# A hybrid attention, mLSTM and PEER layer on one core: 32 first products ahead in place of 28, four of them at the hand-over, and 18 lower parts on GpSimd

## The chip, the core and the metric

The kernel runs on one core of a Trainium2 chip. The metric is the device time of one execution in microseconds. Three timed executions of the kernel before gave a median of 1732.3 us (1725.78 to 1736.87). TensorE is called PE below, VectorE DVE, ScalarE ACT, GpSimd POOL, and SyncE, which issues most DMAs, SP.

## The reference, cut to what matters

The layer has an attention part and an mLSTM part, which come first and which the change doesn't touch. What follows them is PEER: for each token and each of 8 heads, two lists of 16 best sub-keys are ranked, their 256 sums are ranked again, and the 16 best pairs name 16 of 16384 experts.

```
def peer(h, w_pq, sub_keys, expert_u, expert_v):
    ...
        q = (xb @ w_pq).reshape(PEER_BLOCK, PEER_HEADS, 2, PEER_DKH)
        s = jnp.einsum('thpd,hpkd->thpk', q, sub_keys).astype(jnp.float32)
        sv, si = lax.top_k(s, PEER_TOPK)
        cand = (sv[:, :, 0, :, None] + sv[:, :, 1, None, :]).reshape(PEER_BLOCK, PEER_HEADS, -1)
        ...
        best, pos = lax.top_k(cand, PEER_TOPK)
        eidx = jnp.take_along_axis(cidx, pos, axis=-1)
        g = jax.nn.softmax(best, axis=-1)
        act = jax.nn.gelu(jnp.einsum('thkd,td->thk', expert_u[eidx], xb).astype(jnp.float32), approximate=False)
        return jnp.einsum('thk,thkd->td', (g * act).astype(xb.dtype), expert_v[eidx])
```

There are 512 tokens, 1024 channels, 8 heads, 128 keys to a list and 16384 experts.

## The kernel before

Of the four tiles of 128 tokens, tiles 1 to 3 (384 tokens) take PEER densely. The 16384 experts are 128 chunks of 128. For chunk c the **first product** multiplies the chunk of `expert_u` by the 384 tokens (`dense_u`, 24 matmuls of 384 columns, into the one PSUM buffer `u`); Gelu follows on ACT; `weigh` multiplies by the gates of the chunk (DVE, L1271); the **second product** multiplies by the chunk of `expert_v` and adds into six PSUM banks `o` (`dense_v`, 18 matmuls of 512 columns, L1283). Every operand is a pair of a rounded upper part (a copy on ACT, L218) and a lower part (the difference, L219), and `mm3` issues three matmuls for a pair of operands (upper by upper, L255; upper by lower, L256; lower by upper, L257). `split` makes both parts; its last argument is the engine of the difference, DVE if it isn't given. Tile 0 takes PEER sparsely: its lists are ranked by DVE (`tile0`, the generator `late`), and then 256 rows of `expert_u` and `expert_v` are gathered and used one after the other (`gathered`, the generator `gath`).

In time the program has these stages after attention:

- The query products of tiles 1 to 3 (to about 483 us), in which DVE begins to rank (`best16`: MAX8, FIND_INDEX8, MATCH_REPLACE8, MAX8, FIND_INDEX8).
- **Routing** (to about 743 us). Two calls of `weave` mix three strands each, in the given proportions: the ranking on DVE (`first`, `second`), the work of tile 0 on PE, and the first products ahead (`pre`). `second` also makes the gates: one-hot tables on DVE (L1181 to L1186), products on PE (`g`, L1196), evictions on ACT (L1198) into one of two buffers `sg`, and stores to `gd` in HBM in four quarters (L1203, issued by ACT). CFG `f` holds the weights of the strands and how many first products go with each; CFG `pre` is how many are done ahead in all. Outside of `manual_schedule` a scheduler orders each engine's instructions; inside it they stand as they are written.
- **The hand-over.** The gates of the first four chunks come back from `gd` (`load_g`, L1249), the first chunks of `expert_v` are loaded (`load_v`, L1254) into a ring of two buffers `vt`, chunk 0 is weighed and split, and the second products begin. The first buffer of `vt` lies on the last quarter of the buffer `sg` that the last gates are stored from.
- **Second products alone**: while c is below PRE - 1, the chunk's first product is already done. `turn` issues the 47 steps of `late` here, evenly spaced from L0 to G0 (CFG `l`).
- **Pairs**: one first product and one second product for each chunk, with the gathers of tile 0 spread between them.

SP issues its DMAs in order and waits, in order, for what each of them needs. A step of `late` fetches the next list (64 KB from `sc0d`, L1293) into a ring of two buffers and ranks the one before.

Of the kernel before, what the change touches and what calls it, by code (L numbers as in the profile page):

```python
# [49 lines left out]
ENDED = object()  # L50
CFG = dict(nv=2, r=8, l=(0, 34, 124), pre=28, f=(17, 7, 7, 27, 2, 4), oa=2, og=2, gt=2, a=(0, 2), ps=(('g', 2), ('j', 1), ('b', 2), ('s', 1)), w=(22, 22, 22), ko=(4, 5, 6, 7, 0, 1, 2, 3), m=(5, 7, 4, 7, 4, 4, 1), ne=lambda v, g: g, sc=lambda k, n: n == 256 or k % 2, wq=lambda nc: nc.sync, we=lambda i, v, g: g)


class Arena:
# [71 lines left out]
def body(ctx, tc, nc, x_t, ctx_t, cc, w_ada_t, w_ada_n, w_in, w_uq, w_ukv, w_out, w_pq, keys_t,  # L126
# [90 lines left out]
    def split(hi, lo, src, eng=V):  # L217
        A.activation(hi, src, AF.Copy)  # L218
        eng.tensor_tensor(lo, src, f32(hi), op=OP.subtract)  # L219
# [820 lines left out]
    PRE = CFG["pre"]  # L1040
    utr, uhr, ulr = ar.ring("ut", 2, [KD, P]), ar.ring("uh", 3, [4, P], F32R), ar.ring("ul", 3, [4, P], F32R)
    gep = []
# [7 lines left out]
    def split_u(c_, half):  # L1050
        if c_ < P and (c_, half) not in us:
            us[c_, half] = uhr.next(), ulr.next()
            split(*us[c_, half], uts[c_][:, 4 * half:4 * half + 4])

    def dense_u(c_, half):
        if c_ < P and (c_, half) not in fired:
# [163 lines left out]

    def tail0():
        yield from tile0_q()
        yield from pre

    weave((first(), 52), (tile0_x(), CFG["f"][0]), (islice(pre, CFG["f"][1]), CFG["f"][2]))
    obr, ogr = ar.ring("ob", 1, [8, P, 2], BF), ar.ring("og", CFG["og"], [2, 8, P, 2], F16)
    sgr = ar.ring("sg", 2, [P, 32])
    weave((second(), 170), (tail0(), CFG["f"][3]), (islice(pre, CFG["f"][4]), CFG["f"][5]))
    assert len(gep) == PRE
    front.close()  # L1230
    pso = pool(ctx, "pso", 1, **PS)
    ob = [pso.tile([P, 512], F32, name="o%d" % i) for i in range(6)]
# [140 lines left out]

    with tc.manual_schedule():
        NV = len(vtr.v)
        load_g(0)
        for c_ in range(NV):
            load_v(c_)
        load_g(4)
        weigh(0)  # L1380
        weigh_lo(0)
        split_v(0, 0)
        split_v(0, 1)
        for c_ in range(P):
            if c_ == PRE:
                ar.give(*["gp%d" % i for i in range(PRE)])
                tl.update(rows=ar.ring("rows", CFG["r"], [D]), act=ar.take("act", [P]), acc=ar.take("acc", [D]),
                          h2t=ar.take("h2t", [D]))
                nc.scalar.dma_start(tl["h2t"], h0d)
            dense_u(c_ + 1, 0)  # L1390
            split_u(c_ + 2, 0)
            dense_u(c_ + 1, 1)
            split_u(c_ + 2, 1)
            load_u(c_ + 3)
            turn(c_, 1)
            weigh(c_ + 1)
            if c_ < P - 1:
                dense_v(c_, 0)
            turn(c_, 2)
            split_v(c_ + 1, 0)  # L1400
            if c_ < P - 1:
                dense_v(c_, 1)
            else:
                for g in range(3):
                    for half in range(2):
                        dense_v(c_, half, (g,))
            split_v(c_ + 1, 1)
            weigh_lo(c_ + 1)
            load_v(c_ + NV)
            if c_ % 4 == 3:  # L1410
                load_g(c_ + 5)
            turn(c_, 3)
        for _ in late:
            pass
        for _ in gath:
            pass
# [93 lines left out]
```

## Time and profile before

| | |
|---|---|
| median of three executions | 1732.3 us |
| the profiled execution, its own time | 1736.11 us |
| its span | 1734.3 us |
| PE busy | 1629.1 us (94%) |
| DVE busy | 1332.7 us (77%) |
| ACT busy | 735.3 us (42%) |
| POOL busy | 443.6 us (26%) |
| share of the chain that ended last | PE 72%, DVE 17%, ACT 4%, DMA 4% |

Busy shares are means over stages that have different limits, so the stages have to be read one by one. The profiled execution is 3.8 us above the median, and 1.8 us of its time lie outside of its span.

### The profile page before, as it was taken

To read this page: it belongs to the slowest core of one execution; us is meant where nothing else is said; L and a number is where in the kernel's file an instruction comes from. 1 tells how busy PE (TensorE), PEld (TensorE's weight loads), DVE (VectorE), ACT (ScalarE), POOL (GpSimd) and SP (SyncE) were. 2 spreads that over 40 slices of the span, in tenths; PEclk is the share of its full clock that TensorE was granted. 3 is DMA by queue.
4 is the path that set the end of the run, shared out by engine and by line. 5 is a ranking of instruction groups with operands and counts; after the bars stand their busy time and mean duration, and the time that the engine had idled before them with its cause. 6 is when DMAs were issued, how large, how long until landed. Compare 5 with 4: busy or idle time off the path is not lost.

```text
span 1734.3 us, 25190 instructions
## 1 busy us (share of the span) xinstructions
PE 1629.1 (94%) x9119; PEld 1412.4 (81%) x9119; DVE 1332.7 (77%) x2857; ACT 735.3 (42%) x1404; POOL 443.6 (26%) x339
## 2 busy tenths in 40 slices
PE   6889999998988999969899999999999999999988
PEld 4669854588968989857689999999999999999977
DVE  6896165556899997958876887888888888888874
ACT  4563544434345545534353433333333333334322
POOL 6621400033400000000101333333333434444311
PEclk8999988999999999989999999999999999999989
DMA  8456301133314757565777999999999999999962
GB/s 340 145 184 218 104 25 37 31 110 122 119 50 170 267 214 256 204 202 162 260 237 214 341 321 335 336 328 322 325 339 322 318 343 331 323 335 334 314 226 82
DMA packets 155244, 400.92 MB, mean 231 GB/s; under 512 B 13424, under 2 KB 70192, under 8 KB 150000
## 3 DMA queue, kind: packets, MB, share of 16 engines
q1 hardware_dynamic: 108320, 232.05, 39.0%
q0 software_dynamic: 36864, 134.23, 22.5%
q10 hardware_dynamic: 9936, 33.03, 4.9%
q8 instruction: 71, 1.16, 0.3%
q14 instruction: 53, 0.43, 0.1%
HBM read 367.28 MB, written 31.99 MB: 230 GB/s over the span
## 4 chain that ended last, share of the span: by engine, by line
PE 72%; DVE 17%; ACT 4%; DMA 4%; issue 2%; POOL 0%; ACTq 0%; SPq 0%; DVEq 0%
PE o L1283 27%; PE u L255 9%; PE u L257 9%; PE u L256 9%; PE j L255 2%; PE j L256 2%; PE j L257 2%; DVE sp L219 2%; PE s L846 1%; DVE sp L1186 1%; PE s L847 1%; PE g L1196 1%; ACT sp L218 1%; DMA sp<-in_exp_ut 1%; DMA sp<-in_w_ada_t 1%
## 5 line engine op out<-in xcount | busy, mean ns | idle before, releaser
L218 ACT ACTIVATE sp<-sp 128x512 fp32r<-128x512 f32 (+2 forms) x674 | 406.4, 637 | 465.5 <-PE u L256 257.5
L1283 PE MATMUL o<-sp 128*128 128x512 f32 x2304 | 550.1, 393 | 21.1 <-ACT sp L218 14.9
L219 DVE TENSOR_TENSOR sp<-sp,sp 128x512 fp32r<-128x512 f32 (+1 forms) x650 | 407.6, 658 | 158.7 <-ACT sp L218 158.6
L1283 PEld LDWEIGHTS o<-sp 128*128 128x128 f32 x2304 | 432.1, 189 | 113.4 <-ACT sp L218 15.8
L255 PE MATMUL u<-sp,sp 128*128 128x384 f32 x1024 | 349.2, 341 | 14.1 <-ACT sp L1269 7.8
L257 PE MATMUL u<-sp,sp 128*128 128x384 f32 x1024 | 347.8, 340 | 6.7 <-DVE sp L219 6.7
L256 PE MATMUL u<-sp,sp 128*128 128x384 f32 x1024 | 346.1, 338 | 0.0
L1347 POOL DMA_INDIRECT sp<-in_exp_u,sp x128 | 137.2, 1072 | 679.2 <-PE o L1283 360.0
L255 PEld LDWEIGHTS u<-sp,sp 128*128 128x128 f32 x1024 | 194.0, 189 | 20.9 <-ACT sp L1074 8.4
L1347 POOL DMA_INDIRECT sp<-in_exp_v,sp x128 | 151.9, 1187 | 222.3 <-DVE sp L1323 204.9
L257 PEld LDWEIGHTS u<-sp,sp 128*128 128x128 f32 x1024 | 193.7, 189 | 9.0 <-DVE sp L219 7.9
L256 PEld LDWEIGHTS u<-sp,sp 128*128 128x128 f32 x1024 | 193.8, 189 | 3.9
L219 POOL TENSOR_TENSOR sp<-sp,sp 128x2048 fp32r<-128x2048 f32 (+1 forms) x24 | 96.5, 4024 | 264.6 <-ACT sp L218 264.6
L1323 DVE SCALAR_TENSOR_TENSOR sp<-sp 128x1024 f32<-128x1024 f32 x127 | 162.5, 1279 | 0.2
L1311 DVE CUSTOM_DVE_ANT_0 sp<-sp 128x1024 f32<-128x1024 f32 x128 | 155.6, 1215 | 0.0
L257 PE MATMUL j<-sp,sp 128*128 128x256 f32 (+2 forms) x448 | 140.7, 314 | 5.0 <-DVE sp L398 5.0
L255 PE MATMUL j<-sp,sp 128*128 128x256 f32 (+2 forms) x448 | 143.0, 321 | 1.7 <-ACT sp L218 0.9
L256 PE MATMUL j<-sp,sp 128*128 128x256 f32 (+2 forms) x448 | 141.0, 315 | 0.0
L1269 ACT ACTIVATE sp<-u 128x384 f32<-128x384 f32 x100 | 49.2, 492 | 173.4 <-PE u L257 160.5
L1271 DVE TENSOR_TENSOR sp<-sp,sp 128x384 f32<-128x384 f32 x107 | 61.2, 572 | 63.2 <-ACT sp L1269 46.3
L257 PEld LDWEIGHTS j<-sp,sp 128*128 128x128 f32 x448 | 84.6, 189 | 7.5 <-DVE sp L398 5.7
L255 PEld LDWEIGHTS j<-sp,sp 128*128 128x128 f32 x448 | 84.8, 190 | 6.0 <-issue 1.7
(343 smaller groups left out, 1804.3 us busy)
## 6 DMA issues: line engine op xcount, KB each, us to landing
sp<-in_exp_ut SPq DMA_DIRECT2D x128, 512.0 KB, 5.4
sp<-in_exp_v SPq DMA_DIRECT2D x128, 512.0 KB, 6.3
gd<-sp ACTq DMA_DIRECT2D x48, 512.0 KB, 4.5
sp<-gd SPq DMA_DIRECT2D x32, 768.0 KB, 9.7
sp<-in_w_ada_t SPq DMA_DIRECT2D x38, 512.0 KB, 4.4
sp<-in_w_pq SPq DMA_DIRECT2D x16, 1024.0 KB, 5.1
sp<-in_w_in SPq DMA_DIRECT2D x8, 1024.0 KB, 5.2
sp<-in_w_out SPq DMA_DIRECT2D x8, 1024.0 KB, 4.8
```

Source lines behind the costliest of these rows:

```text
L218: A.activation(hi, src, AF.Copy)
L219: eng.tensor_tensor(lo, src, f32(hi), op=OP.subtract)
L255: T.matmul(ps, lh, rh, start=(first and i == 0), stop=False)
L256: T.matmul(ps, lh, rl, start=False, stop=False)
L257: T.matmul(ps, ll, rh, start=False, stop=(last and i == n - 1))
L846: T.matmul(p_[:, c0:c1], qn[:, h, o], knT[:, h, c0:c1], start=True, stop=False)
L1269: A.activation(ge, pu.pop(c_), AF.Gelu)
L1271: V.tensor_tensor(blk(w), blk(ge), gts[c_ // 4][:, :, c_ % 4], op=OP.mult)
L1283: T.matmul(ob[2 * g + half], l_[:, g * P:g * P + P], fl(r_), start=(c_ == 0 and i == 0), stop=(c_ == P - 1 and i == 2))
L1311: V.tensor_tensor_reduce(out=u, in0=u, in1=h2t, scale=1.0, scalar=0.0, op0=OP.mult, op1=OP.add, accum_out=act[:, j:j + 1])
L1323: V.scalar_tensor_tensor(acc, v, act[:, j:j + 1], acc, op0=OP.mult, op1=OP.add)
L1347: G.indirect_dma_start(out=r_, out_offset=None, in_=table, in_offset=bass.IndirectOffsetOnAxis(ap=col, axis=0))
```

## The change

PRE becomes 32 and `hold` is 4: 28 first products still lie in the two calls of `weave` (now 9, 17 and 2 in its strands, before 7, 19 and 2), and four more are written into the hand-over, each followed by two steps of `late`. The loads of the first two chunks of `expert_v` are written ahead of these four, the first two loads of gates behind them. For the first nine chunks `split_u` takes the difference on POOL. In CFG `l` the second number goes from 34 to 36. The table PLACE, which says where each buffer lies in SBUF, changes for buffers of this stage; the buffers `vt`, `sg` and `gt` lie where they lay.

```
-CFG = dict(nv=2, r=8, l=(0, 34, 124), pre=28, f=(17, 7, 7, 27, 2, 4), ...
+CFG = dict(nv=2, r=8, l=(0, 36, 124), pre=32, hold=4, f=(17, 9, 9, 25, 2, 4), ...
...
     def split_u(c_, half):
         if c_ < P and (c_, half) not in us:
             us[c_, half] = uhr.next(), ulr.next()
-            split(*us[c_, half], uts[c_][:, 4 * half:4 * half + 4])
+            split(*us[c_, half], uts[c_][:, 4 * half:4 * half + 4], G if c_ < CFG["f"][1] else V)
...
     def tail0():
         yield from tile0_q()
-        yield from pre
+        yield from islice(pre, PRE - CFG["hold"] - CFG["f"][1] - CFG["f"][4])
...
-    assert len(gep) == PRE
+    assert len(gep) == PRE - CFG["hold"]
...
     with tc.manual_schedule():
         NV = len(vtr.v)
-        load_g(0)
+
         for c_ in range(NV):
             load_v(c_)
+        for _ in pre:
+            for _ in range(2):
+                done[1] += 1
+                next(late)
+        split_v(0, 0)
+        split_v(0, 1)
+        load_g(0)
         load_g(4)
         weigh(0)
         weigh_lo(0)
-        split_v(0, 0)
-        split_v(0, 1)
```

The lines of the changed kernel are one higher than before from PLACE on. On SP, from the last loads of `expert_ut` on, the kernel before has this order at the hand-over (`gd` are gates, `sc0d` lists of tile 0):

```order
L1048 DMA sp_1707<-in_exp_ut 128x1024 x15
L1249 DMA sp_58<-gd 128x12x128
L1254 DMA sp_58<-in_exp_v 128x1024 x2
L1249 DMA sp_58<-gd 128x12x128
L1293 DMA sp_3680<-sc0d 128x128
```

The changed kernel has this one there, behind the same 15 loads of `expert_ut`:

```order
L1255 DMA sp_58<-in_exp_v 128x1024 x2
L1049 DMA sp_1707<-in_exp_ut 128x1024
L1294 DMA sp_3680<-sc0d 128x128
L1294 DMA sp_58<-sc0d 128x128
L1049 DMA sp_1707<-in_exp_ut 128x1024
L1294 DMA sp_3680<-sc0d 128x128
L1294 DMA sp_58<-sc0d 128x128
L1294 DMA sp_3680<-sc0d 128x128
L1294 DMA sp_58<-sc0d 128x128
L1294 DMA sp_3680<-sc0d 128x128
L1294 DMA sp_58<-sc0d 128x128
L1250 DMA sp_58<-gd 128x12x128 x2
```

The load of the first gates has moved from the front of this row to its end, behind two loads of `expert_ut` and eight fetches of lists.

On DVE the kernel before has this order at the hand-over (128x2048 are one-hot tables, 128x384 the weighed chunk, 128x512 lower parts of `expert_u` and then of `expert_v`):

```order
L1186 TENSOR_TENSOR sp_58<-sp_58 128x2048 x2
L219 TENSOR_TENSOR sp_3676<-sp_1707,sp_3676 128x512
L1271 TENSOR_TENSOR sp_58<-sp_1707,sp_58 128x384
L219 TENSOR_TENSOR sp_3676<-sp_58,sp_3676 128x384
L219 TENSOR_TENSOR sp_3676<-sp_58,sp_3676 128x512 x2
```

The changed kernel has this one after its last one-hot table; the row goes on in the same way, with two rankings between the lower parts of one held product and those of the next, up to seven rankings:

```order
L1187 TENSOR_TENSOR sp_58<-sp_58 128x2048 x2
L220 TENSOR_TENSOR sp_3676<-sp_1707,sp_3676 128x512 x2
L988 MAX sp_58<-sp_3680 128x8
L989 MAX_INDEX sp_1707<-sp_58,sp_3680 128x8
L990 MATCH_REPLACE sp_58<-sp_58,sp_3680 128x128
L991 MAX sp_58<-sp_58 128x8
L992 MAX_INDEX sp_1707<-sp_58 128x8
L220 TENSOR_TENSOR sp_3676<-sp_1707,sp_3676 128x512 x2
```

Rankings of tile 0 now stand between the lower parts of held products, the first of them ahead of the second product's lower parts.

## Rows read from the trace of the kernel before

**Rows 1.** Windows by stage: span, then busy us per engine, granted clock, DMA share, GB/s.
```profile
480.00:640.00 160.00, 142.08 (x1093) 129.58 (x1092) 157.25 (x595) 81.04 (x169) 0.00 (x0) 0.98 0.51 179
640.00:743.00 103.00, 99.75 (x874) 92.27 (x871) 84.47 (x89) 56.22 (x110) 0.00 (x0) 1.00 0.59 212
743.00:757.00 14.00, 0.27 (x1) 0.27 (x1) 1.40 (x3) 1.90 (x4) 0.00 (x0) 0.60 0.92 303
757.00:881.00 124.00, 116.83 (x485) 91.93 (x486) 106.40 (x362) 48.82 (x93) 7.71 (x8) 0.98 0.68 213
881.00:1660.00 779.00, 779.00 (x3942) 709.43 (x3941) 631.61 (x967) 304.97 (x568) 281.10 (x248) 1.00 0.92 319
```
**Rows 2.** Chain of work that ended last, at the hand-over: start, us, what.
```profile
742.35 1.09 ACT sp L1198 x2
...
745.84 5.58 DMA gd<-sp
...
751.49 4.54 DMA sp<-in_exp_v
...
756.73 4.52 PE o L1283 x9
```
**Rows 3.** Timeline of SP's queue at the hand-over.
```profile
747.15 0.38 SPq L1249 DMA_DIRECT2D sp<-gd  x1
751.49 0.81 SPq L1254 DMA_DIRECT2D sp<-in_exp_v  x2
```
**Rows 4.** Waits of SP's queue from 735 to 790: us in total, times, longest.
```profile
SPq L1254 <- DMA gd<-sp: 3.9, 1, 3.9
```
**Rows 5.** Timeline of DVE behind the hand-over, in brackets the idle time before.
```profile
754.76 0.56 DVE L1271 TENSOR_TENSOR sp<-sp,sp 128x384 f32<-128x384 f32 x1 [16.91 <-DMA sp<-gd]
...
763.02 0.29 DVE L987 MAX8 sp<-sp 128x8 f32<-128x128 f32 x1
...
764.60 0.54 DVE L1271 TENSOR_TENSOR sp<-sp 128x384 f32<-128x384 f32 x1
```
**Rows 6.** Timeline of PE at the first pair.
```profile
881.41 0.33 PE L255 MATMUL u<-sp,sp 128*128 128x384 f32 x1
...
885.60 4.28 PE L1283 MATMUL o<-sp 128*128 128x512 f32 x18
889.72 0.33 PE L255 MATMUL u<-sp,sp 128*128 128x384 f32 x1
```
**Rows 7.** Timeline of PE at the first product ahead.
```profile
490.02 0.69 PE L257 MATMUL u<-sp,sp 128*128 128x384 f32 x1 [4.77 <-DVE sp L219]
```
**Rows 8.** Groups by line: POOL's lower parts of 128x512, busy us, mean ns, idle before.
```profile
L219 POOL TENSOR_TENSOR sp<-sp,sp 128x512 fp32r<-128x512 f32 x6 | 10.5, 1760 | 3.8 <-ACT sp L218 3.8
```
**Rows 9.** The line L219 on POOL: min/median/max ns, first and last start.
```profile
L219 POOL TENSOR_TENSOR sp<-sp,sp x24: 1295/4584/7429, 24.7 to 465.1; 128x2048 fp32r<-128x2048 f32 x18, 128x512 fp32r<-128x512 f32 x6
```
**Rows 10.** Timeline of POOL, its last lower part.
```profile
465.06 4.58 POOL L219 TENSOR_TENSOR sp<-sp,sp 128x2048 fp32r<-128x2048 f32 x1 [5.29 <-ACT sp L218]
```
**Rows 11.** Timeline of DVE from 450 to 482.
```profile
454.63 0.46 DVE L938 TENSOR_TENSOR sp<-sp 128x48 f32<-128x48 f32 x4
465.34 4.87 DVE L938 TENSOR_TENSOR sp<-sp 128x8 f32<-128x8 f32 x7
```
**Rows 12.** Groups by line, of DVE and of ACT: busy us, mean ns, idle before.
```profile
L219 DVE TENSOR_TENSOR sp<-sp,sp 128x512 fp32r<-128x512 f32 x514 | 344.4, 687 | 153.9 <-ACT sp L218 153.8
L218 ACT ACTIVATE sp<-sp 128x512 fp32r<-128x512 f32 x520 | 324.3, 627 | 433.0 <-PE u L256 257.5 <-PE o L1283 153.3 <-DMA sp<-in_exp_v 10.4
L1074 ACT ACTIVATE sp<-u 128x384 f32<-128x384 f32 x28 | 13.7, 488 | 35.7 <-PE u L257 32.5 <-PE j L1135 3.1
```
**Rows 13.** The fetches of lists, L1293: issue to landing, whole run.
```profile
DMA to landing us min/median/max: 1.9/3.9/7.7
```
**Rows 14.** The loads of gates, L1249: issue to landing, whole run.
```profile
DMA to landing us min/median/max: 5.9/9.7/13.3
```
**Rows 15.** Waits of PE from 756 to 890: us in total, times, longest.
```profile
PE o L1283 <- DVE sp L219: 5.9, 8, 1.4
```

More of the change, by code (lines that the diff above doesn't have):

```diff
@@ L44 @@
     24640, 24608, 1405, 16476, 912, 1278, 1549, 16468, 1166, 1421, 1318, 1956, 16688, 1006, 1830,
[2 rows of a table removed]
[2 rows of a table added]
     856, 16497, 1599, 880, 28672, 1038, 576, 704, 24736, 24800, 24968, 25000, 24768, 24888, 16560,
[2 rows of a table removed]
[3 rows of a table added]
 ENDED = object()
-CFG = dict(nv=2, r=8, l=(0, 34, 124), pre=28, f=(17, 7, 7, 27, 2, 4), oa=2, og=2, gt=2, a=(0, 2), ps=(('g', 2), ('j', 1), ('b', 2), ('s', 1)), w=(22, 22, 22), ko=(4, 5, 6, 7, 0, 1, 2, 3), m=(5, 7, 4, 7, 4, 4, 1), ne=lambda v, g: g, sc=lambda k, n: n == 256 or k % 2, wq=lambda nc: nc.sync, we=lambda i, v, g: g)
+CFG = dict(nv=2, r=8, l=(0, 36, 124), pre=32, hold=4, f=(17, 9, 9, 25, 2, 4), oa=2, og=2, gt=2, a=(0, 2), ps=(('g', 2), ('j', 1), ('b', 2), ('s', 1)), w=(22, 22, 22), ko=(4, 5, 6, 7, 0, 1, 2, 3), m=(5, 7, 4, 7, 4, 4, 1), ne=lambda v, g: g, sc=lambda k, n: n == 256 or k % 2, wq=lambda nc: nc.sync, we=lambda i, v, g: g)
 class Arena:
```

9 rows, old and new, of the table PLACE are left out of this document.

## The prediction

> **What bounds the kernel now.** I read the windows by stage first. In the pairs PE is busy for all of the 779 us at full clock, and DVE for 631.6 of them [rows 1], so PE bounds that stage and what leaves PE there leaves the time. A first product takes 4.19 us of it (881.41 to 885.60) and a second product 4.12 us (885.60 to 889.72) [rows 6]. In routing both are near their limit: up to 640 us DVE is busy for 157.3 of 160 us and PE for 142.1; after that PE for 99.8 of 103 us and DVE for 84.5 [rows 1]. The one wide hole of PE is the hand-over, 14 us with 0.27 us of work at a mean granted clock of 0.60 [rows 1]. The chain there runs from the last evictions of gates (end 743.44) over the stores by ACT, the last of which lands at 751.42, to the load of `expert_v`, and PE starts at 756.73 [rows 2]. The first gates were requested at 747.15, before the last store had landed, and used at 754.76 [rows 3, 5]; the request for `expert_v` stood 3.9 us waiting for that last store [rows 4], since its buffer lies on what is stored. So the reader is to see that SP's queue is open until 751.42 only for what doesn't need that buffer.
>
> **Part 1: four first products fewer in the pairs.** 100 pairs become 96, and four second products stand alone in their place: 4 x 4.19 = -16.8 us [rows 6]. The gathers of tile 0 now lie on 90 chunks instead of 93. DVE's 631.6 of 779 us become some 3% denser in them, and PE's 779 of 779 still cover that; without that cover each chunk would run at DVE's pace, which is under 8.31 us by these rows. Counted at nothing.
>
> **Part 2: the hand-over, and what SP and DVE have queued there.** The load of `expert_v` now stands at the head of SP's queue, so all behind it waits until the last store has landed: two loads of `expert_ut`, eight fetches of lists, and then only the gates. I count from 743.44. The store lands at +8.0 [rows 2]. Two issues of `expert_v` take 0.81 us, and the issues behind them about 0.38 us each [rows 3], so the first list is asked for at about +9.6. It lands 1.9 to 7.7 us later [rows 13]; three loads of half a megabyte stand ahead of it, so I take the median of the run, 3.9: +13.5. DVE ranks it before it makes the lower parts of the second held product. One ranking is 1.6 us (763.02 to 764.60) [rows 5], one lower part 0.69 us [rows 12], so PE, which has had the first held product and two matmuls of the second for a cover, goes on at +15.8. It has then stood for about ten microseconds. After the hole before, the first nine matmuls of 512 columns took 4.52 us [rows 2], and nine of eighteen at full clock are 2.06 [rows 6]; I add these 2.5 us. The 22 matmuls left are 22/24 of 4.19, 3.84 us: +22.1.
>
> The third and fourth held products each wait for Gelu of the one before, since the copies of the next upper parts stand behind it on ACT: 0.49 + 0.63 + 0.69 = 1.8 us [rows 12], and then 3.84 us of PE. The rankings between them (two of 1.6 us) fit into that. So the third ends at +27.7, and the fourth has its first lower part at +29.5 and its second at +30.2. The fifth ranking after it (1.6 us) frees the buffer for the eighth fetch, and only behind that fetch are the gates asked for: about +32.2. They landed 7.6 us after their request before (747.15 to 754.76) [rows 3, 5]; that gives +39.8. The product by the gates (0.56 us) [rows 5] and the copy (about 0.5 us, nearest row Gelu of the same width [rows 12]) bring the second products to +40.9. Before it was +13.3 (756.73 less 743.44) [rows 2], so the stage costs **+27.6 us**. Its ends: with the fastest fetch (-2.0), the fastest load of gates, 5.9 us (-1.7) [rows 14] and no slow clock (-2.5), +21.4; with the slowest fetch (+3.8) and the median load of gates, 9.7 us (+2.1), +33.5. I take the middle sum, since every duration in it but the fetch is the nearest one in place. PE does its four products, but stands for about as long as before again, ahead of the second products. The slow clock at their start is in both kernels.
>
> **Part 3: second products alone.** Seven rankings, 7 x 1.6 = 11.2 us of DVE, have left a stage in which DVE is busy for 106.4 of 124 us [rows 1] and PE waits for it 8 times, 5.9 us in all [rows 15]. The other 39 steps keep nearly their old spacing, with the same tables and the same first gathers, and four chunks more have their waits. I take a quarter of the 5.9 us: **-1.5 us**; at most -5.9, and +0.9 (four chunks more at 5.9 us in 27) if nothing is saved.
>
> **Part 4: routing, and the lower parts on POOL.** The first product ahead stood 4.77 us at its first lower part, which was queued on DVE behind rankings. POOL's queue holds nothing ahead of it by then: -4.8 us [rows 7]. DVE gives up 18 x 0.69 = 12.4 us [rows 12]. Against that stands what POOL's instructions do to DVE. Seven additions on DVE that should take about 0.8 us (four larger ones took 0.46 [rows 11]) took 4.87 us when POOL had begun a lower part of 4.58 us 0.3 us before [rows 10, 11]. So an operation of DVE with two operands in SBUF stands until POOL's is over. A lower part of 128x512 takes POOL 1.30 us at least and 1.76 in the mean [rows 8, 9]. The hold for one is therefore between 0 (DVE is at a reduction or a MAX8, which read one operand) and 1.76 us; I take 0.8, a little under the middle, since such operations are mixed among the additions. 18 x 0.8 = 14.4 us eat the 12.4 us; the 2.0 us that remain pass to the end of routing by about half, as PE is the fuller engine after 640 us [rows 1]. Together -4.8 + 1.0, about **-4 us**, with ends at -11 (no hold, and half of the 12.4 us counts) and +14.5 (each is held for 1.76 us, and all of it counts: 31.7 - 12.4 - 4.8).
>
> By the Trainium skill, SBUF — State Buffer, section "Who interferes with whom", a DVE instruction with two inputs in SBUF contends with a GpSimd instruction that reads SBUF, and whichever starts first keeps the shared ports for the whole instruction. The row of 4.87 us beside 4.58 us agrees. Applied to every one of the 18, it would make part 4 the +14.5 us of the upper end, and it speaks against this half of the change; that result is the second rival below.
>
> **Sum.** -16.8 + 27.6 - 1.5 - 4 = +5.3 us. On the profiled execution's 1736.1 us that is 1741.4; that execution is 3.8 us above the median, so the forecast is 1732.3 + 5.3 = 1737.6, about **1738 us**: no change that a measurement can tell (under 1% for this kernel).
>
> **Rival 1: the held products fill the hole.** If SP's queue isn't closed by the last store, because `expert_v` can be loaded before it, lists come at once. The first held product, of which some 18 matmuls stand behind the last gate products, ends at about +2.5, when ACT has issued its last store (745.84 [rows 2]); with 1.8 us of Gelu, copy and lower part and 3.84 us of PE each, the second ends at +8.1 and the third at +13.8, the fourth has its lower parts at +16.3, and behind a ranking, the request, the gates' 7.6 us and 1.1 us more the second products start at about +27, +13.7 on before. With -11 in routing the sum is -16.8 + 13.7 - 1.5 - 11 = -15.6: 1717 us. The place of the buffer speaks against it [rows 4]; 12%, of which some more than half ends beyond 1% faster if the waits of part 3 go too.
>
> **Rival 2: POOL holds DVE up.** Each of the 18 lower parts holds a two-operand operation of DVE for the whole of its 1.76 us, and routing, where DVE has 2.7 us of slack in 160 [rows 1], ends 14.5 us later. The sum is -16.8 + 27.6 - 1.5 + 14.5 = +23.8: 1756 us. It goes over 1% (+17.3 us) from a hold of about 1.4 us each. For it is the row of 4.87 us [rows 11]; against it, that POOL often will begin while DVE is at a MAX8 or a reduction, and that the mean of 1.76 us is itself stretched by such meetings (1.30 is the least [rows 9]). 15%.
>
> **Rival 3: routing gains all it can** and the hand-over is as in part 2: -16.8 + 27.6 - 1.5 - 11 = -1.7, 1731 us. 23%; it lies within 1%.
>
> **Chances.** The forecast has 50%. Range: from 1720 (rival 1 for the most part) to 1755 (rival 2, and the upper end of part 2). Faster by over 1% comes from the better half of rival 1, 8%; slower by over 1% from rival 2 and from the upper ends of parts 2 and 4 together, 16%; within 1%, 76%.
>
> **What would show it.** The profile after should have the first request of `expert_v` waiting for the stores of the gates, the first list of tile 0 landing some 13 us after the last eviction, PE idle for about ten microseconds within the held products and again for six to eight ahead of the second products, and the second products starting about 41 us after the last eviction of gates. In routing the first product ahead should not stand for its lower part, and additions on DVE beside POOL's lower parts should read 1 to 2 us. 96 pairs should take 8.31 us each. I am wrong if the lists or the gates are on their way before the last store has landed, or if DVE's additions don't stretch.

## The result, and the profile after

The changed kernel took 1752.99 us in the median of 4 runs (1752.39 to 1758.67), the kernel before 1733.59 beside it (1725.78 to 1736.87, 4 runs): a ratio of 1.0119, 95% interval 1.0087 to 1.0152. It is slower by 1.2%, within the range, but not the "no change" of the forecast. The profiled execution has a span of 1756.9 us against 1734.3; 3.8 of these 22.6 us are a stretch ahead of the query products that the change doesn't touch and that varies between runs (the query products end at 475 to 488 us in the profiles here).

The windows by stage of the kernel after answer to [rows 1]: span, then busy us per engine (PE, PEld, DVE, ACT, POOL), granted clock, DMA share, GB/s.

```profile
480.00:640.00 160.00, 140.35 (x985) 126.53 (x984) 151.93 (x590) 74.64 (x151) 27.00 (x18) 0.94 0.43 150
640.00:761.80 121.80, 114.28 (x1013) 104.96 (x1012) 93.57 (x102) 64.95 (x131) 0.00 (x0) 1.00 0.63 227
761.80:799.00 37.20, 18.11 (x88) 15.86 (x86) 16.13 (x65) 6.54 (x13) 0.00 (x0) 0.80 0.51 165
799.00:940.00 141.00, 136.35 (x568) 109.93 (x569) 110.72 (x339) 55.75 (x105) 7.71 (x8) 0.96 0.64 205
940.00:1690.00 750.00, 750.00 (x3796) 683.07 (x3794) 615.67 (x932) 294.02 (x547) 279.79 (x248) 1.00 0.93 327
```

In the first 160 us PE has started 985 matmuls where it had started 1093, and POOL's 18 lower parts are new. The second row is 19 us longer, with the work that is still missing. The hand-over is 37 us long, half of it without PE.

The exact stages, read from where instructions begin and end (last matmul of the query products; end of the last eviction of gates; first matmul of `o`; first matmul of `u` behind it; start of the last matmul of `u`), each from one profiled execution:

| us | before | after | difference | forecast |
|---|---|---|---|---|
| routing | 260.55 | 275.03 | +14.5 | -4 |
| hand-over | 13.30 | 37.40 | +24.1 | +27.6 |
| second products alone (four more: 4 x 4.12 = 16.5) | 124.68 | 139.24 | +14.6, so -1.9 without these | -1.5 |
| pairs (four fewer; with the 16.5 above) | 836.83 | 802.37 | -34.5, so -18.0 | -16.8 |

The chain of work that ended last, at the hand-over, answers to [rows 2] (start, us, what):

```profile
760.66 1.10 ACT sp L1199 x2
...
763.46 4.84 DMA gd<-sp
...
769.78 5.50 DMA sp<-sc0d
...
776.96 0.68 DVE sp L220
...
783.51 0.63 ACT sp L219
...
792.64 5.32 DMA sp<-gd
...
799.15 5.93 PE o L1284 x14
```

The chain goes over the last store, the first list, its ranking and the lower part behind it, then over Gelu, copy and lower part of the next products, and at the end over the fetch of the gates. SP's queue there, against [rows 3] (its timeline) and [rows 4] (its waits from 755 on):

```profile
768.45 0.81 SPq L1255 DMA_DIRECT2D sp<-in_exp_v  x2
...
769.78 0.96 SPq L1294 DMA_DIRECT2D sp<-sc0d  x2
...
778.69 13.90 SPq L1294 DMA_DIRECT2D sp<-sc0d  x6
792.64 1.23 SPq L1250 DMA_DIRECT2D sp<-gd  x2
```
```profile
SPq L1255 <- DMA gd<-sp: 16.7, 1, 16.7
```

The queue opens 6.7 us after the last eviction (768.45 less 761.75), and the gates, which had been the first request, are the last. PE's timeline shows what that cost (idle time and releaser in brackets):

```profile
777.69 0.69 PE L258 MATMUL u<-sp,sp 128*128 128x384 f32 x1 [11.28 <-DVE sp L220]
...
790.12 0.45 PE L256 MATMUL u<-sp,sp 128*128 128x384 f32 x1 [1.10 <-ACT sp L219]
...
799.15 3.36 PE L1284 MATMUL o<-sp 128*128 128x512 f32 x7 [4.22 <-ACT sp L219]
```

That stage went nearly as forecast (PE's last wait is 4.22 us, where six to eight were expected). Routing did not. PE's timeline at its head, with the wait that was gone and the one that came [rows 7]:

```profile
489.24 0.45 PE L258 MATMUL u<-sp,sp 128*128 128x384 f32 x1 [0.15 <-POOL sp L220]
...
497.20 0.66 PE L256 MATMUL u<-sp,sp 128*128 128x384 f32 x1 [3.85 <-ACT sp L1075]
...
501.09 2.07 PE L847 MATMUL s<-sp,sp 128*128 128x512 f32 x2 [1.62 <-DVE sp L990]
```

The 4.77 us ahead of the first product are 0.15 now, as forecast. But 3.85 us follow ahead of the second one. And DVE beside POOL, against [rows 10, 11]: first POOL's timeline, then DVE's.

```profile
542.86 1.33 POOL L220 TENSOR_TENSOR sp<-sp,sp 128x512 fp32r<-128x512 f32 x1 [4.45 <-ACT sp L219]
```
```profile
541.36 0.17 DVE L939 TENSOR_TENSOR sp<-sp 128x48 f32<-128x48 f32 x1
...
542.98 1.42 DVE L939 TENSOR_TENSOR sp<-sp 128x32 f32<-128x32 f32 x3
544.32 0.32 DVE L954 MAX8 sp<-sp 128x8 f32<-128x54 f32 x2
```

An addition alone takes 0.17 us; three of them, of which the first begins 0.12 us behind POOL's lower part, take 1.42. The first of the three has 1.26 of that and ends as POOL's part does (544.24 and 544.19). Of the 93 additions of line L939 in 480 to 590 us the median is 0.18 us and the longest 1.31. Beside the 18 lower parts 12 of DVE's operations in routing are longer by over 0.15 us than the median of the same operation in the run lower_on_dve (below), by 10.4 us together: ten with two inputs, one scaling and one conversion. None of the 41 MAX8, FIND_INDEX8 and MATCH_REPLACE8 that begin beside a lower part is among them.

### The profile page after: what moved, and what is told of

It reads as the page before. It is cut to its first block, busy times and chain, and to the rows that moved or that the text cites. A ratio compares the mean times of both kernels' runs of the same rounds, so it can differ in the third digit from the quotient of the medians.

```text
span 1756.9 us, 25185 instructions
## 1 busy us (share of the span) xinstructions
PE 1644.5 (94%) x9119; PEld 1421.2 (81%) x9119; DVE 1328.5 (76%) x2839; ACT 736.0 (42%) x1404; POOL 467.7 (27%) x357
## 4 chain that ended last, share of the span: by engine, by line
PE 72%; DVE 15%; DMA 4%; ACT 3%; issue 1%; POOL 0%; SPq 0%; ACTq 0%; DVEq 0%
PE o L1284 28%; PE u L256 9%; PE u L258 9%; PE u L257 9%; PE j L256 2%; PE j L257 2%; PE j L258 2%; DVE sp L1187 2%; PE g L1197 1%; PE s L847 1%; PE s L848 1%; PE j L1136 1%; DVE sp L939 1%; DMA sp<-in_w_ada_t 1%; PE j L865 1%
## 5 line engine op out<-in xcount | busy, mean ns | idle before, releaser
L219 ACT ACTIVATE sp<-sp 128x512 fp32r<-128x512 f32 (+2 forms) x674 | 406.2, 638 | 472.0 <-PE u L257 259.7
L220 DVE TENSOR_TENSOR sp<-sp,sp 128x512 fp32r<-128x512 f32 (+1 forms) x632 | 395.0, 656 | 166.3 <-ACT sp L219 164.1
L220 POOL TENSOR_TENSOR sp<-sp,sp 128x512 fp32r<-128x512 f32 (+1 forms) x42 | 123.1, 2937 | 350.2 <-ACT sp L219 328.8
```

## The experiments

All kernels carry the four held products of the change unless the text says otherwise. Stage times are read as in the table above, each from one profile; ratios are to the kernel before, run on the same chip. Most of these kernels have another table PLACE as well. Two of them, no_parts and copies_on_dve, leave a part of the computation out.

| run | routing | hand-over | median us | ratio, 95% interval |
|---|---|---|---|---|
| the change | 275.0 | 37.4 | 1752.99 | 1.0119 (1.0087 to 1.0152) |
| lower_on_dve | 263.5 | 39.1 | 1743.77 | 1.0039 (1.0018 to 1.0061) |
| old_shares | 260.0 | 38.1 | 1744.91 | 1.0035 (1.0011 to 1.0059) |
| old_shares_pool | 270.4 | 37.2 | 1753.14 | 1.0093 (1.0061 to 1.0125) |
| twin_parts | 275.8 | 38.7 | 1756.21 | 1.0121 (1.0097 to 1.0145) |
| read_write | 273.4 | 38.1 | 1753.73 | 1.0091 (1.0072 to 1.0109) |
| write_only | 263.5 | 39.0 | 1744.76 | 1.0035 (1.0019 to 1.0051) |
| no_parts | 263.2 | 37.5 | 1739.96 | 1.0026 (1.0009 to 1.0044) |
| copies_on_dve | 262.2 | 38.5 | 1741.37 | 1.0026 (1.0012 to 1.0040) |
| gates_first | 263.7 | 39.3 | 1740.81 | 1.0025 (1.0010 to 1.0041) |
| lists_later | 263.5 | 29.1 | 1732.98 | 0.9980 (0.9961 to 0.9999) |
| loads_ahead | 262.1 | 26.0 | 1728.09 | 0.9945 (0.9926 to 0.9963) |
| new_hand_over | 260.7 | 18.4 | 1722.26 | 0.9922 (0.9892 to 0.9952) |

old_shares and the last four have the shares and DVE's lower parts of before, so their routing, 260.0 to 263.7, shows how far that stage varies between profiles of nearly one order of instructions: about 4 us.

### Which part of the change costs routing its time

**lower_on_dve** undoes POOL's part.

```diff
-            split(*us[c_, half], uts[c_][:, 4 * half:4 * half + 4], G if c_ < CFG["f"][1] else V)
+            split(*us[c_, half], uts[c_][:, 4 * half:4 * half + 4], V)
```

> The changed kernel with one edit undone: the lower parts of the first nine products are made on VectorE again; 9, 9, 25 shares and the four held products stay. Two theories of the 14.5 us that the routing (last query product to last gate eviction) grew from 260.6 to 275.0. Theory P, GpSimd's parts: the order around them puts ScalarE's copies of the ranking ahead of the products' upper parts, TensorE waits and works at half clock; then the routing here is 258 to 264 and the time 1736 to 1742. Theory S, the shares: two more products stand ahead of tile 0 in the first stretch (2 x 4.2 us of TensorE), tile 0 and its queries come later, and TensorE's waits at half clock follow; then the routing is 270 to 277 and the time 1747 to 1754. I hold S the likelier. Theory H, that GpSimd's tensor work holds VectorE up, gives the same as P here, but with VectorE's ranking operations shorter than in the changed kernel.

**old_shares** undoes the shares as well.

```diff
-            split(*us[c_, half], uts[c_][:, 4 * half:4 * half + 4], G if c_ < CFG["f"][1] else V)
+            split(*us[c_, half], uts[c_][:, 4 * half:4 * half + 4], V)
...
-f=(17, 9, 9, 25, 2, 4)
+f=(17, 7, 7, 27, 2, 4)
```

> The changed kernel with the routing of the kernel before: shares 7, 7, 27 and VectorE's lower parts, so TensorE's order is row for row that of before as far as the last gate; 28 products ahead there, four held between the last gates and the second products as in the change. The routing should be 260 to 262 us. If the four terms of the sum are as measured in the changed kernel (pairs -17, hand-over +24, second products alone -2), the time is 1733.6 + 5 = 1737 to 1741, and the change's loss beyond that is all routing. If the hand-over's loss itself came from what the routing left in the queues, the second products would start less than 30 us after the last eviction and the time would fall under 1730.

**old_shares_pool** undoes the shares and keeps POOL, for seven products.

```diff
-f=(17, 9, 9, 25, 2, 4)
+f=(17, 7, 7, 27, 2, 4)
```

> As the run with the old shares 7, 7, 27, but with the lower parts of the first seven products on GpSimd; four held products as in the change. Theory P (GpSimd's parts cost the routing) expects a routing of 270 to 277 us and a time of 1750 to 1755, 10 to 15 above the run with the old shares alone. Theory S (the shares 9, 9, 25 cost it) expects 258 to 264 us and 1733 to 1742, equal to that run within 4 us. An interaction of the two would show as a routing between, 264 to 270.

With POOL less without it, routing is 11.5 us longer at the new shares (275.0, 263.5) and 10.4 at the old ones (270.4, 260.0); the new shares less the old are 3.5 and 4.6 us, about what a profile varies by. So theory P holds, and S, which I had held the likelier, falls. The times of lower_on_dve and old_shares came out 2 to 4 us above what was expected; the kernel before took 1737.05 us on their chip, 3.5 more than beside the change. But P had two things in it, since the scheduler orders the other engines anew around POOL's parts: the order, and what POOL's instructions do while they run.

### The hold by itself

**twin_parts** adds POOL's work to lower_on_dve and takes none from DVE.

```diff
+    tw = ar.take("tw", [4, P], F32R)
...
-            split(*us[c_, half], uts[c_][:, 4 * half:4 * half + 4], G if c_ < CFG["f"][1] else V)
+            split(*us[c_, half], uts[c_][:, 4 * half:4 * half + 4])
+            if c_ < CFG["f"][1]:
+                G.tensor_tensor(tw, uts[c_][:, 4 * half:4 * half + 4], f32(us[c_, half][0]), op=OP.subtract)
```

> The kernel of the run lower_on_dve (VectorE makes the lower parts of the first nine products, shares 9, 9, 25, four held) with 18 instructions added: GpSimd subtracts the same lower parts once more, into a spare tile that nobody reads. The order of instructions on TensorE, VectorE, ScalarE and SyncE is the same in both, so what differs is what GpSimd's instructions do to the others while they run. In the changed kernel VectorE's operations with two inputs in SBUF took 10.4 us longer in all, near GpSimd's parts, than the same ones of lower_on_dve. Theory H, the hold: it recurs here, and since VectorE is busy over 98% of the first 100 us, the routing goes from 263.5 to 270 to 276 and the time to 1750 to 1756. Theory O, the order that the scheduler makes around GpSimd's parts: the order is as before, so the routing stays at 262 to 266 and the time at 1741 to 1746.

Routing went from 263.5 to 275.8 us. Here is the same place in both on DVE's timeline, lower_on_dve first:

```profile
539.67 0.28 DVE L267 TENSOR_TENSOR sp<-sp 128x128 f32<-128x128 f32 x1
539.87 0.60 DVE L973 TENSOR_TENSOR sp<-sp 128x432 f32<-128x432 bf16 x1
540.39 0.20 DVE L939 TENSOR_TENSOR sp<-sp 128x40 f32<-128x40 f32 x1
```

twin_parts:

```profile
540.62 1.38 DVE L267 TENSOR_TENSOR sp<-sp 128x128 f32<-128x128 f32 x1
541.91 0.60 DVE L973 TENSOR_TENSOR sp<-sp 128x432 f32<-128x432 bf16 x1
542.43 1.27 DVE L939 TENSOR_TENSOR sp<-sp 128x40 f32<-128x40 f32 x1
```

and POOL's timeline there:

```profile
540.12 3.53 POOL L1057 TENSOR_TENSOR sp<-sp,sp 128x512 fp32r<-128x512 f32 x2 [7.09 <-ACT sp L219]
```

Each of POOL's two instructions holds one operation with two inputs for a microsecond, and two of them take 3.53 us in place of the 2.6 that two of the shortest [rows 9] would. I set each of DVE's operations in routing beside the same one of lower_on_dve: 14 are longer by over 0.15 us, by 11.2 us together. Not all of the 14 have two inputs: a scaling of 128x768 went from 0.62 to 1.64 us and a conversion of 128x64 from 0.18 to 0.48. By the end of that stretch DVE runs 11.3 us late, and the last eviction is 12.3 us late. So the hold is enough for the loss, with no change of order; theory O isn't needed here.

It is not shown that the order costs nothing in the kernels where it did change. In old_shares_pool only 8 of DVE's operations are longer by over 0.15 us than in old_shares, by 5.2 us together, and yet its routing is 10.4 us longer than that of old_shares. About half of that loss doesn't show as longer operations of DVE, and what else it is, the new order or lower parts that POOL has later, wasn't found.

**read_write** and **write_only** have one order on the other four engines, and differ in whether POOL reads.

```diff
-            split(*us[c_, half], uts[c_][:, 4 * half:4 * half + 4], G if c_ < CFG["f"][1] else V)
+            split(*us[c_, half], uts[c_][:, 4 * half:4 * half + 4])
+            if c_ < CFG["f"][1]:
+                u_ = uts[c_][:, 4 * half:4 * half + 4]
+                G.tensor_tensor(u_, u_, u_, op=OP.subtract)
```

> The kernel of the run lower_on_dve with 18 instructions of GpSimd added: as soon as a half of a product's exp_ut tile has been split, GpSimd subtracts it from itself in place (nobody reads it again before the next load). GpSimd reads and writes as many elements as in the changed kernel. On the other four engines the order is that of lower_on_dve but for 5 matmuls and 6 operations of VectorE. If the hold through reads holds (the run with the parts made twice: routing 263.5 to 275.8, 14 of VectorE's operations longer by 11.2 us in all), the routing is 270 to 277 and the time 1749 to 1757. If that loss came from buffers that GpSimd kept from their next user, it is under 268 here, since the upper and lower parts are not touched.

```diff
-                u_ = uts[c_][:, 4 * half:4 * half + 4]
-                G.tensor_tensor(u_, u_, u_, op=OP.subtract)
+                G.memset(uts[c_][:, 4 * half:4 * half + 4], 0.0)
```

> As the run read_write, but GpSimd's 18 instructions fill the same half tiles with zeros, so that they write and don't read; the order on the other four engines is exactly that of read_write. If VectorE is held only while GpSimd reads, the routing is 262 to 267 us (lower_on_dve 263.5), no operation of VectorE is longer, and the time is 1740 to 1746. If any work of GpSimd on SBUF holds VectorE, the routing is as in read_write, or less by the share by which a fill is shorter than a subtraction: 267 to 276.

POOL's group of read_write (busy us, mean ns, idle before):

```profile
L1057 POOL TENSOR_TENSOR sp<-sp 128x512 f32<-128x512 f32 x18 | 22.4, 1251 | 83.4 <-DVE sp L220 83.4
```

of write_only:

```profile
L1056 POOL MEMSET sp<- 128x512 f32 x18 | 9.5, 526 | 87.8 <-DVE sp L220 87.7
```

and DVE's additions L939 (min/median/max ns, first and last start) of read_write:

```profile
L939 DVE TENSOR_TENSOR sp<-sp x79: 121/185/1043, 496.1 to 585.5; 128x32 f32<-128x32 f32 x21, 128x16 f32<-128x16 f32 x17, 128x48 f32<-128x48 f32 x11, 128x64 f32<-128x64 f32 x8
```

of write_only:

```profile
L939 DVE TENSOR_TENSOR sp<-sp x85: 134/184/234, 481.1 to 587.1; 128x32 f32<-128x32 f32 x23, 128x16 f32<-128x16 f32 x19, 128x48 f32<-128x48 f32 x12, 128x64 f32<-128x64 f32 x8
```

With reads, additions of 0.18 us go up to 1.04 and routing is 9.9 us longer; with writes alone none is over 0.23 us, though 23 of DVE's operations with two inputs begin during a fill, and routing is 263.5, what it was without POOL. A fill takes 0.42 of the time of a subtraction; if any work of POOL counted, 0.42 x 9.9 = 4.2 us should have been seen. By the Trainium skill, SBUF — State Buffer, section "Who interferes with whom", a DVE instruction with two SBUF inputs contends with a GpSimd instruction that reads SBUF, "not with one that only writes it". These two runs agree with both halves.

### Why the work taken from DVE bought nothing

**no_parts** lets neither engine make the lower parts.

```diff
             us[c_, half] = uhr.next(), ulr.next()
-            split(*us[c_, half], uts[c_][:, 4 * half:4 * half + 4], G if c_ < CFG["f"][1] else V)
+            if c_ < CFG["f"][1]:
+                us[c_, half] = us[c_, half][0], us[c_, half][0]
+                A.activation(us[c_, half][0], uts[c_][:, 4 * half:4 * half + 4], AF.Copy)
+                return
+            split(*us[c_, half], uts[c_][:, 4 * half:4 * half + 4])
```

> The changed kernel (shares 9, 9, 25, four held) in which the lower parts of exp_ut in the first nine products are made by nobody: the product takes the upper part in their place, as many matmuls as ever, so a part of the computation is left out. TensorE's order is that of the changed kernel but for 45 of 9277 matmuls. Theory O, the order with its early first product, the wait behind it and the half clock: they are all still here, and the routing stays at 270 to 276. Theory H, the hold: without it VectorE also has 12.4 us less to do than in lower_on_dve, and the routing falls to 252 to 260, the time to 1731 to 1739. A value between, 262 to 268, would say that both count.

The result lies between, at 263.2, which by the expectation says that both count. Against the changed kernel, with almost its order, that is -11.8 us: the hold once more, now taken away. Against lower_on_dve it is nothing, although DVE has 18 lower parts less to make. But no_parts has the order of the changed kernel, not that of lower_on_dve, so this nothing is the sum of two things: what freed DVE time gives and what the new order takes. No run takes the lower parts from DVE and keeps the order. The windows from the last query product on show where they went; first lower_on_dve, its first 40 us and the sum over routing:

```profile
483.70:503.70 20.00, 14.25 (x59) 11.24 (x58) 19.55 (x100) 5.51 (x11) 0.00 (x0) 0.83 0.21 60
503.70:523.70 20.00, 18.40 (x110) 15.37 (x109) 19.69 (x92) 14.52 (x26) 0.00 (x0) 1.00 0.16 53
...
sum 263.50, PE 241.15 PEld 221.03 DVE 239.87 ACT 139.74 POOL 0.00; mean PE 30.14 PEld 27.63 DVE 29.98 ACT 17.47 POOL 0.00
```

and no_parts:

```profile
478.90:498.90 20.00, 14.60 (x53) 9.71 (x51) 17.41 (x98) 5.26 (x10) 0.00 (x0) 0.72 0.21 60
498.90:518.90 20.00, 19.03 (x94) 15.85 (x93) 18.49 (x105) 13.13 (x24) 0.00 (x0) 0.85 0.18 52
...
sum 263.20, PE 245.83 PEld 224.19 DVE 228.62 ACT 139.96 POOL 0.00; mean PE 30.73 PEld 28.02 DVE 28.58 ACT 17.50 POOL 0.00
```

DVE is busy for 11.3 us less and idle for as much more. PE has the first product sooner, then stands 3.5 us; the granted clock of the two stretches is 0.72 and 0.85, where lower_on_dve has 0.83 and 1.00, with 147 matmuls in 40 us where that has 169. DVE in turn waits for a product `s` of tile 0 that PE makes late; its waits in routing, first lower_on_dve, then no_parts (us in total, times, longest):

```profile
DVE sp L850 <- PE s L848: 0.5, 1, 0.5
DVE sp L850 <- PE s L848: 3.6, 2, 3.1
```

The wait of 3.1 us is there in the changed kernel and in old_shares_pool too, the other two with the order around POOL's parts, so the order has a price. In the changed kernel PE's wait is the 3.85 us shown above. There ACT stands at the copy of a ranking; behind it are the second product's upper parts, the load of a table (1.28 us) and the first product's Gelu (ACT's timeline, the changed kernel):

```profile
493.91 0.26 ACT L949 ACTIVATE sp<-sp 128x64 f32<-128x64 uint32 x1 [5.04 <-DVE sp L939]
...
496.66 0.49 ACT L1075 ACTIVATE sp<-u 128x384 f32<-128x384 f32 x1
```

**copies_on_dve** tries whether that wait is the reason.

```diff
-        A.activation(sif[:, :, 0], x_[:, :, 0], AF.Copy, scale=128.0)
-        A.activation(sif[:, :, 1], x_[:, :, 1], AF.Copy)
+        V.tensor_scalar(sif[:, :, 0], x_[:, :, 0], 128.0, None, op0=OP.mult)
+        V.tensor_copy(sif[:, :, 1], x_[:, :, 1])
```

> The kernel of the run no_parts (the lower parts of exp_ut in the first nine products made by nobody, the upper part in their place, so a part of the computation is left out) with one edit: in the ranking of pairs the two copies of the lists' indices (L949 and L950 of the changed kernel) are made by VectorE instead of ScalarE; the scheduler's order shifts with that, so this is no test of one wait alone. In no_parts VectorE's 12.4 us fewer bought nothing (routing 263.2 against 263.5). Theory W: they were lost because ScalarE stood some 5 us at these copies with the Gelu of the first product behind them, TensorE stood 3.5 us for that and went on at a lower clock; without it the routing falls to 252 to 259 us and the time to 1730 to 1736. Theory T: TensorE's own work and its other waits set the routing once VectorE has time to spare; then the routing stays at 261 to 266 and the time at 1737 to 1744.

The wait went (0.58 us in its place), and routing stayed at 262.2, as theory T has it. PE's waits in routing (us in total, times, longest) show one for DVE instead, some 7 us later:

```profile
PE s L847 <- DVE sp L990: 5.6, 1, 5.6
```

So ACT's copies alone did not keep routing long, and theory W as it stood falls. Since a longer wait came so soon behind the place of the first, and DVE's wait for `s` stayed (3.3 us), the run doesn't show what routing would be without such a wait.

### The hand-over

**lists_later** and **gates_first** each change one thing in old_shares.

```diff
         for _ in pre:
-            for _ in range(2):
-                done[1] += 1
-                next(late)
+            pass
```

> The kernel of the run old_shares (routing of before, four held) with one edit in the hand-over: no steps of tile 0's lists stand among the held products; they follow in the loop of pairs, as in the kernel before. SyncE's queue is as it was: both rows of exp_v first, waiting for the last gate store, then two fetches of exp_ut, then the gates. If the rankings ahead of the lower parts are the larger share of the slow hand-over (38.1 us), it falls to 24 to 29 us and the time to 1727 to 1736. If the closed queue is the larger share, it stays over 31 us and the time within 7 us of old_shares.

```diff
+        load_g(0)
         for c_ in range(NV):
             load_v(c_)
...
         split_v(0, 1)
-        load_g(0)
         load_g(4)
```

> The kernel of the run old_shares with one edit in the hand-over: the first fetch of gates goes ahead of everything else on SyncE there, while the steps of tile 0's lists stay among the held products. The fetch took 5.3 us at the end of the chain, behind the last fetch of a list. If it is only that link, the second products start 30 to 34 us after the last eviction (38.1) and the time is 1735 to 1741. If the closed queue as a whole was the cause, they start under 26; if the rankings set the pace, 34 or more.

Without the lists' steps the hand-over is 9.0 us shorter (38.1 to 29.1). With the gates first and the lists in place it is not shorter at all (39.3), so the place of the gates is not what sets the pace. Its chain still goes over the last store and the first list's fetch behind the closed queue, and then over a ranking and over the Gelus, copies and lower parts between the held products:

```profile
745.85 6.08 DMA gd<-sp
...
753.40 5.55 DMA sp<-sc0d
```

The lists' steps thus cost by their late fetch and by their rankings together. What is left in lists_later shows in its chain: a fetch of `expert_ut` behind the closed queue.

```profile
746.26 5.35 DMA sp<-in_exp_ut
...
751.70 0.64 ACT sp L219
```

**new_hand_over** writes the whole stage anew, with the old shares and no POOL; **loads_ahead** is the same without the first piece of the diff.

```diff
             if c_ + 2 < PRE:
                 load_u(c_ + 2)
+            if PRE - CFG["hold"] <= c_ < PRE - 1:
+                split_u(c_ + 1, 0)
+                split_u(c_ + 1, 1)
...
+        next(pre)
+        next(pre)
+        load_g(0)
         for c_ in range(NV):
             load_v(c_)
-        for _ in pre:
-            for _ in range(2):
-                done[1] += 1
-                next(late)
+        next(pre)
         split_v(0, 0)
         split_v(0, 1)
-        load_g(0)
-        load_g(4)
         weigh(0)
         weigh_lo(0)
+        for _ in pre:
+            pass
+        load_g(4)
```

> The routing of the kernel before (7, 7, 27, VectorE's parts), four held products, and the hand-over written anew: the fetch of the first gates (load_g(0)) goes ahead of both rows of exp_v and behind only two fetches of exp_ut; no steps of tile 0's lists stand among the four products; a product's parts are made ahead of the Gelu of the one before. If the hand-over was slow because SyncE waited for the last gate store with everything behind it, and the lists' rankings stood ahead of the lower parts, then the second products start 19 to 24 us after the last gate eviction (13.3 before, 37.4 in the changed kernel), the four pairs give back 16.8, and the time is 1721 to 1729, below both kernels. If the chain of a product's Gelu, copy and lower part alone sets the pace of the held products, they still start 30 us or more behind and the time is 1732 or more.

> The kernel of the run new_hand_over without one of its edits: a product's parts are again made behind the Gelu of the one before. The rest stays: two fetches of exp_ut, then the gates, then the rows of exp_v on SyncE's queue, and no list steps. In lists_later the gaps between the held products were the wait for exp_ut behind the closed queue and some 1.8 us of Gelu, copy and lower part each. If the chain of Gelu, copy and lower part is worth its 1.8 less the 1.0 that a Gelu alone takes for each of three products, the second products start 20 to 22 us after the last eviction (18.4 in new_hand_over, 29.1 in lists_later) and the time is 1722 to 1730; if it is worth more than the queue's order, 24 to 28 and 1728 to 1733.

PE's timeline in new_hand_over, from the last gates to the second products (a wait like the second stands once more, at 750.75):

```profile
745.73 0.45 PE L256 MATMUL u<-sp,sp 128*128 128x384 f32 x1 [1.01 <-ACT sp L1078]
...
755.76 0.44 PE L256 MATMUL u<-sp,sp 128*128 128x384 f32 x1 [0.58 <-ACT sp L1078]
...
760.04 2.24 PE L1287 MATMUL o<-sp 128*128 128x512 f32 x9
```

in loads_ahead (a wait like the first stands once more, at 752.94):

```profile
747.01 0.44 PE L256 MATMUL u<-sp,sp 128*128 128x384 f32 x1 [1.10 <-ACT sp L219]
...
761.73 0.69 PE L256 MATMUL u<-sp,sp 128*128 128x384 f32 x1 [3.97 <-ACT sp L219]
...
768.62 1.55 PE L1284 MATMUL o<-sp 128*128 128x512 f32 x6
```

The order of the queue, written together with the last product's new place behind `split_v` and `weigh`, is worth 3.1 us (29.1 to 26.0), and the parts made ahead of Gelu 7.6 (26.0 to 18.4), more than the 2 to 4 I had expected: in loads_ahead the last product's copies also stand behind those of `expert_v` and the first weights, 3.97 us, and PE goes on at a granted clock of 0.50 (761.7 to 765.0), the lower of its two levels. In new_hand_over it is 1.00 there (755.7 to 760.0). new_hand_over is faster than both kernels, 0.9922 of the one before. There the second products start 18.4 us after the last eviction, 5.1 later than before, and the pairs are four fewer.

## Why the prediction was right and wrong

**Part 1, four pairs fewer: right.** -18.0 us against -16.8. A pair still takes 8.30 us (938.39 to 946.69), and DVE's denser gathers stay hidden (615.67 of 750 us, PE 750.00).

**Part 2, the hand-over: right, +24.1 against +27.6.** The second products start 37.4 us after the last eviction, forecast 40.9. The queue waits for the last store, the first list comes behind it, the gates come last, and PE's two waits are there, 11.28 and 4.22 us. Three terms were mis-sized and partly cancel: the queue opened at +6.7 us, not +8.0, the first list took 5.50 us, not 3.9, and the gates were at DVE 5.3 us after their request, not 7.6. What I hadn't weighed is how the cost divides. Taking out the lists' steps alone gives back 9.0 us (old_shares to lists_later), asking for the gates first alone nothing (gates_first), since the lists, their rankings and the lower parts behind them still come late.

**Part 3, second products alone: right**, -1.9 against -1.5.

**Part 4, routing: wrong, and more than the whole error.** Forecast -4, measured +14.5: 18.5 us too low, of which the other three parts, each a little too high, hide 5.1. The time is within the range all the same, 2 us below its upper end, and that end was there for rival 2 and the upper end of part 2, not for this sum. The step that failed is the netting: "18 x 0.8 = 14.4 us eat the 12.4 us". It set the hold against the 12.4 us and the 4.77 us of the first wait, and gave the order that the scheduler makes around POOL's parts no price. The hold itself was sized about right: 10.4 us over DVE's operations in the changed kernel and 11.2 in twin_parts, about 0.6 each, not 0.8. It is paid in full where the order is kept (12.3 us of routing in twin_parts). The 12.4 us and the 4.77 us, together with the new order, bought nothing. Going from the kernel before to the change by way of the runs: new shares +3.0 (260.55 to 263.5, about what profiles vary by), the lower parts taken off DVE, with the order that came of it, -0.3 (263.5 to 263.2, no_parts), POOL's instructions +11.8 (263.2 to 275.0); together +14.5. Whether freed DVE time is worth nothing here, or is worth something that the new order takes back, stays open; the waits of PE and DVE in no_parts speak for the second.

The count of PE's matmuls fits with the hold. Within 80 us of the last query product the trace has 417 matmuls started on PE before, 405 in lower_on_dve, 412 in no_parts and 404 in copies_on_dve, whether DVE has the lower parts to make or not; there are 358 in twin_parts and 356 after. So a late DVE reaches PE at once, while a DVE with time to spare gained PE at most 7 matmuls in these two runs. Which of PE's other waits takes over is shown for two kernels, Gelu behind ACT's copies in no_parts and a ranking on DVE in copies_on_dve. What would have to go together for routing to get shorter than 260 us wasn't found.

**The rivals.** Rival 2 came near the time (1756 us) and had the +14.5, with the right mechanism and the wrong make-up, so its number is luck in part: it took a hold of 1.76 us for each part and a gain of 17.2 us against it; measured are some 0.6, and almost none once the new order is counted in. Rival 1's hand-over, second products at +27, fails for the reason given (the place of the buffer). With the hand-over written anew it is beaten: +18.4. Rival 3, all of the gain in routing, is refuted by no_parts, where even without any hold it isn't there (263.2 us, 260.55 before). The 16% for slower by over 1% was too little, since I gave the gain of freed DVE time no chance of coming to nothing.

## What to carry to other kernels

Work moved to GpSimd beside a VectorE that is 98% busy must be priced by what GpSimd reads: here each subtraction of 128x512 cost 0.66 us of the stage (11.8 us for 18), nearly what VectorE takes to make it (0.69). What an engine is relieved of counts only if the next engine's row shows that it waits for nothing else, and a scheduler's new order can take it back; count it at zero as one end of the range. A stage that hands over through one in-order queue is won by the order of requests and copies: the hand-over with the same four products took 37.4 us or 18.4. With the routing of before, the four products paid in the three runs whose hand-over took 29.1 us or less, and not in those with 38 to 39.

## What the runs showed of the hardware that was not expected

GpSimd fills 128x512 in 0.53 us, and subtracts in place in 1.25 in the mean; the fill beside VectorE's two-input additions left them at 0.23 us at most. The hold goes both ways: 15 of GpSimd's 18 lower parts in the changed kernel took 1.26 to 1.36 us, and the other three 1.69, 2.27 and 3.92, the last beside two one-hot tables of VectorE of 1.21 us each. A wait on TensorE can cost more than its own time: in the changed kernel the granted clock is 0.51 from 497.2 to 501.0 us, behind the wait of 3.85, and 0.50, the lower of the two levels, from 501.0 to 505.0, and two matmuls of L847 took 2.07 us there where the same two took 1.12 before, at 1.00 (497.2 to 501.3).
